# Square sums and factor rows of the norms on TensorE, token halves in the first head, and the last head's output-gate products in its own recursion

## The chip, the cores and the metric

The kernel runs on one core of a Trainium2 chip. The metric is the time of one execution on the device in microseconds (us); the kernel before takes 2332.52 us, the median of three runs (2330.86 to 2333.41). Five engines run side by side, each through its own list of instructions in a fixed order: TensorE (PE: matmuls, PEld: the weight loads beside them), VectorE (DVE), ScalarE (ACT), GpSimd (POOL) and SyncE (SP, which issues most DMAs). An engine that comes to an instruction whose inputs are not there waits, and everything behind it in its list waits too.

## The reference, cut to what matters

```python
def rmsnorm(x, w):
    y = x * lax.rsqrt(jnp.mean(x * x, axis=-1, keepdims=True) + EPS)
    return y * w

def mlstm_mixer(h, ...):                # 4 heads, chunks of 128 tokens, both directions
    proj = h @ w_in                     # q, k, v, output gate, 16 gate columns
    o_gate = sigmoid(proj[..., o3:o4])
    h_fwd, h_bwd = chunkwise recursions over q, k, v and the gates
    hs = h_fwd + h_bwd; hs = hs * lax.rsqrt(mean(hs * hs) + EPS) * norm_w
    return (hs * o_gate) @ w_out

for i in range(2):                      # 1024 tokens, width 1024
    hn = rmsnorm(x, norm_mix_w[i])
    x = x + (mlstm_mixer(hn) if i == 0 else window_attn_mixer(hn))
    x = x + swiglu(rmsnorm(x, norm_ffn_w[i]))      # inner width 2816
return rmsnorm(x, norm_final_w)
```

Everything is in float32. So there are five norms: before the mLSTM (norm 0), before the first feed-forward network (FFN0, norm 1), before the attention (norm 2), before the second (FFN1, norm 3), and at the end.

## The kernel before, in words

**Layout.** `x` lies transposed: eight tiles of 128 features by 1024 tokens. A float32 product is made of three faster ones: both operands are split into a high and a low part (`hnh`/`hnl`, `wh`/`wl`; ACT makes the high part at L187 or L200, DVE or POOL the low part at L201, L205 or L188), and PE runs high-high, low-high and high-low into one PSUM bank.

**A norm.** The factor of a token is a sum over features, that is over partitions. ACT squares the eight `x` tiles; DVE adds the squares into one tile `R` (`norm_square_row`, L285 to L292); PE sums `R` over partitions with one-column matmuls (`norm_sums`, L364); `rsqrt` (L348) makes the factor from the sums by one power on POOL and six small DVE operations, token by token down the partitions (`rcol`); `spread` (L370) turns it into a row over all partitions: DVE multiplies the identity by each column of `rcol`, high and low part (L376, L377), two matmuls with ones follow (L381, L382), ACT copies the result to `R`. The factor is applied to the products, not to their inputs, so matmuls of normed inputs can start before it is known. Norms 1 and 3 are computed while the last output projection before them ends: each finished pair of `x` tiles is made into the FFN's operands (`norm_forms`, L320: `f1`, `f23h`/`f23l`, `f12h`/`f12l`, `f34h`/`f34l`), then squared. The sums and rows are left as two pending steps, which the FFN takes up between its products (`settle`, L441, called at L563 and L574).

**The FFN's start.** `ffn_up` (L536) has seven products of half size per 128 hidden units (`seven`, L525, matmuls at L532). For the first block it runs five products over pairs 0 to 2 first, 45 matmuls, and pair 3 after that.

**The mLSTM.** Each head's inputs come as eight products of 24 matmuls, four for query and key (`qk`: two weights by two token halves) and four for the output gate (`so`), cut into parts of three, and then the values (L476). `m_mix` gives a recursion of steps: `pk` and `pn` matmuls at L212 that wait for DVE and ACT (`cf`, `cp`) and are waited for by them. `weave` (L55) puts the parts of the next head between the steps of the current one. The last head has no next one: its recursion was woven with the output projection of heads 0 and 1 (`out_pair(y01)`, L668), after `take_back` (L708) has fetched and split their kept outputs and `load_x` (L235) has queued the sixteen loads of `x`.

**The order.** The Tile framework's scheduler sets each engine's order from the program's order and a model of its own; buffers come from pools (46 tiles of 128x1032 floats, PSUM banks in phases), so a tile's new use waits for the last reader of the old one.

Of the kernel before, what the change touches and what calls it, by code (L numbers as in the profile page):

```python
# [19 lines left out]
P = 128  # L20
# [61 lines left out]
class Trunk:  # L82
# [58 lines left out]
    def sources(self):  # L141
        h = self.h
        cols = lambda src: [src[:, o:o + D] for o in range(0, src.shape[-1], D)]
        out = [h["m_gate"]]
        for u in range(3 * NH):
# [12 lines left out]
        for u in range(4):  # L158
            att += cols(h["a_out"][u])
        return out + ffn[0] + att + ffn[1]  # L160
# [124 lines left out]
    def norm_square_row(self, d):  # L285
        nc = self.nc
        if not self.seen[0]:
            nc.scalar.activation(self.R, self.x[d], AF.Square)
        else:
            sq = self.unit(name="sq")  # L290
            nc.scalar.activation(sq, self.x[d], AF.Square)
            nc.vector.tensor_tensor(self.R, self.R, sq, op=ALU.add)  # L292
        self.seen = [n + 1 for n in self.seen]

    def norm_direct(self, half):
        nc = self.nc
        V, G = nc.vector, nc.gpsimd
        a, b = (self.slab() for _ in range(2))
        for d in range(KT):
            x = self.xv(d, half)  # L300
            sq = (b if d % 2 else a)[:, d // 2 * HALF:(d // 2 + 1) * HALF]
            if half and d < 6:
                nc.scalar.activation(sq, x, AF.Square)
            else:
                G.tensor_tensor(sq, x, x, op=ALU.mult)
        V.tensor_tensor(a[:, :S], a[:, :S], b[:, :S], op=ALU.add)
        G.tensor_tensor(a[:, S:], a[:, S:], b[:, S:], op=ALU.add)
        yield
        V.tensor_tensor(a[:, :S], a[:, :S], a[:, S:], op=ALU.add)
        V.tensor_tensor(self.Rv(half), a[:, :HALF], a[:, HALF:S], op=ALU.add)  # L310
        yield
# [36 lines left out]
    def rsqrt(self, out, ss, n, tag, w):  # L348
        nc = self.nc
        v = self.t([P, w], F32, tag + "v", 2)  # L350
        g = self.t([P, w], F32, tag + "g", 2)
# [18 lines left out]
    def spread(self, t, n):  # L370
        nc = self.nc
        hi, lo = (self.t2(F32R)[:, :n] for _ in range(2))
        for j in range(n // P):
            o = slice(j * P, (j + 1) * P)
            r = self.rcol[:, t // P + j:t // P + j + 1]
            nc.vector.tensor_scalar(hi[:, o], self.ident, r, None, op0=ALU.mult)  # L376
            nc.vector.scalar_tensor_tensor(  # L377
                lo[:, o], self.ident, r, hi[:, o].bitcast(F32), op0=ALU.mult, op1=ALU.subtract
            )
        rb = self.bank("mx")[:, :n]  # L380
        nc.tensor.matmul(rb, lhsT=self.ones_r, rhs=hi, start=True, stop=False)  # L381
        nc.tensor.matmul(rb, lhsT=self.ones_r, rhs=lo, start=False, stop=True)  # L382
        nc.scalar.activation(self.R[:, t:t + n], rb, AF.Copy)
        return rb
# [51 lines left out]
    def norm_end(self):  # L436
        sums = lambda: [self.norm_sums(half) for half in range(2)]
        rows = lambda: [self.norm_rows(half) for half in range(2)]
        self.pending = [sums, rows]
# [96 lines left out]
    def ffn_up(self, i):  # L536
# [4 lines left out]
        for f in range(NF):  # L541
# [21 lines left out]
            self.settle()  # L563
# [7 lines left out]
            if f:  # L571
                pc = self.bank("mm")
            self.seven(cur, pc, "s1", "t1", **rest)
            self.settle()  # L574
# [93 lines left out]
    def out_pair(self, ys, last=False):  # L668
# [3 lines left out]
        def piece(e, half):  # L672
# [17 lines left out]
            def done(po):  # L690
                x = self.xv(d, half)
                nc.vector.tensor_tensor(x, x, po, op=ALU.add)  # L692
                if last and e % 2 and half:
                    i = e // 2
                    if i == 2:
                        self.first, todo = self.left()
                        for f in todo:
                            f()
                    self.norm_forms(i)
                    for k in (i, i + 4):  # L700
                        self.norm_square_row(k)
                        self.keep_x(k)

# [147 lines left out]
    def m_in(self, hh, t):  # L851
# [4 lines left out]
        def feature(unit, w, half):  # L856
            dst = lambda: t["qk" if unit == 0 else "so"][:, w * S + half * HALF:w * S + (half + 1) * HALF]

            def pairs():
                if w == 0 and half == 0:  # L860
                    t["qk" if unit == 0 else "so"] = self.slab()
                if half == 0:
                    st["w"] = self.w()
                else:
                    self.ahead()
                return self.dense_pairs(st["w"], half)
# [25 lines left out]
        fs = sum((feature(u, w, half) for u in range(2) for w in range(2) for half in range(2)), [])  # L892
        return fs, self.v_parts(value)
# [164 lines left out]
    def mlstm(self):  # L1058
        nc, h = self.nc, self.h
        with ExitStack() as es:  # L1060
# [6 lines left out]
            with self.tc.manual_schedule(engines={mybir.EngineType.Activation}):  # L1067
                sums = [self.norm_direct(half) for half in range(2)]
                for half in range(2):
                    for d in range(KT):  # L1070
                        self.norm_split(d, half)
                        if half and d == 4:
                            next(sums[0])
                    next(gates)
                    next(sums[half])
                next(sums[1])
# [3 lines left out]
            marks = (11, 16, 28, 36, 44)  # L1080
            norms = [lambda: self.norm_sums(0), lambda: self.norm_rows(0), lambda: self.norm_sums(1), lambda: self.norm_rows(1)]
            for i, f in enumerate(ins[0][0]):
                if i in (1, 3, 4, 7):
                    norms.pop(0)()
# [3 lines left out]
            weave(mix[0][0], ins[0][1])  # L1088
            y01, y2 = [[], []], []
            for hh in range(NH):  # L1090
                early, steps, late, y = mix[hh]
                if hh + 1 < NH:
                    weave(steps, ins[hh + 1][0])
                    nxt = mix[hh + 1][0]
                    both = [late[0], nxt[0], late[1], late[2], nxt[1], late[3], late[4], nxt[2], nxt[3]]
                    weave(both, ins[hh + 1][1])
# [10 lines left out]
            self.norm_end()  # L1107
# [247 lines left out]
    def attn(self):  # L1355
# [8 lines left out]
        with self.phase("a", 6, dict(mm=3, sc=2, tp=2, mx=1)):  # L1364
# [45 lines left out]
            self.norm_end()  # L1410
# [98 lines left out]
```

## Time and profile before

| | |
|---|---|
| median of three runs | 2332.52 us |
| the profiled execution | 2334.53 us |
| its span, first to last instruction | 2332.8 us |
| mean granted TensorE clock | 0.982 |
| busy: PE, PEld | 2228.1 us (96%), 1826.9 us (78%) |
| busy: DVE, ACT, POOL | 1421.6 us (61%), 832.8 us (36%), 608.7 us (26%) |

Busy times are shares of the span; the engines overlap. PE has the work that fills the time, so what counts is where PE stands still or runs at its lower clock. The granted clock is given as a share of 2.4 GHz; 0.50 is 1.2 GHz.

### The profile page before, as it was taken

Reading aid. Unit: us, or ns where it says so; the run is one execution under the profiler, and the core shown is the slowest. Engines: PE = TensorE matmul, PEld = TensorE weight load, DVE = VectorE, ACT = ScalarE, POOL = GpSimd, SP = SyncE. Lnnn points to the kernel's source line nnn. Section 1 sums busy time; section 2 is a strip of 40 time slices with the busy share of each in tenths; the row PEclk is TensorE's granted clock in tenths of the full one; section 3 lists DMA queues with packets and bytes.
Section 4 is the critical chain, followed back from the end, with each engine's and each line's share of the span. In section 5 each row is a group of like instructions: output and inputs, shape, how many; then the busy total and the mean of one; then the engine's idle time right before and its main releaser. Section 6 shows DMA issues by size and latency. Waiting matters only on the chain.

```text
span 2332.8 us, 28234 instructions
## 1 busy us (share of the span) xinstructions
PE 2228.1 (96%) x10655; PEld 1826.9 (78%) x10655; DVE 1421.6 (61%) x2603; ACT 832.8 (36%) x1533; POOL 608.7 (26%) x410
## 2 busy tenths in 40 slices
PE   6999998989999999999999998898999999999998
PEld 3889888867888888778878776786788888878887
DVE  5456656678766666592224689878766666653113
ACT  3334445344222222222222577764322222232021
POOL 4312213221111111231343455550111111133043
PEclk9999999998999999999999999999999999999999
DMA  3211114122222222622222444603222222263112
GB/s 114 58 37 46 52 49 145 55 99 82 82 82 82 82 81 77 229 97 86 92 89 85 130 132 135 206 10 116 74 82 81 82 82 82 74 240 119 46 55 73
DMA packets 75961, 216.77 MB, mean 93 GB/s; under 512 B 8320, under 2 KB 14976, under 8 KB 75824
## 3 DMA queue, kind: packets, MB, share of 16 engines
q1 hardware_dynamic: 64216, 177.07, 23.3%
q10 hardware_dynamic: 11608, 37.89, 4.1%
q8 instruction: 84, 1.38, 0.2%
q14 instruction: 53, 0.43, 0.1%
HBM read 159.15 MB, written 55.77 MB: 92 GB/s over the span
## 4 chain that ended last, share of the span: by engine, by line
PE 77%; DVE 8%; issue 5%; DMA 4%; POOL 2%; ACT 2%; SPq 1%; POOLq 0%; ACTq 0%; DVEq 0%
PE mm L532 37%; PE mm L628 18%; PE mm L228 12%; PE mm L476 4%; PE pn L212 2%; DMA raw<-in_a_in_dram 1%; PE sc L1271 1%; POOL wl L188 1%; DVE smd L1286 1%; PE pk L212 1%; DMA slab<-bounce 1%; PE tp L1300 1%; PE mx L1315 1%; ACT e L1280 1%; DVE e L1276 1%
## 5 line engine op out<-in xcount | busy, mean ns | idle before, releaser
L188 POOL TENSOR_TENSOR wl<-raw,wh 128x1024 fp32r<-128x1024 f32 (+2 forms) x96 | 233.7, 2439 | 594.0 <-ACT wh L187 391.2
L628 PE MATMUL mm<-hh,wl 128*128 128x512 f32 (+1 forms) x768 | 289.9, 378 | 4.6 <-POOL wl L188 4.6
L628 PE MATMUL mm<-hh,wh 128*128 128x512 f32 (+1 forms) x768 | 289.0, 379 | 4.3 <-ACT hh L200 3.2
L628 PE MATMUL mm<-hl,wh 128*128 128x512 f32 (+1 forms) x768 | 289.9, 377 | 1.1 <-DVE hl L201 1.1
L579 POOL TENSOR_TENSOR t<-t,R 128x512 f32<-128x512 f32 x44 | 57.4, 1305 | 613.6 <-ACT t L578 613.6
L628 PEld LDWEIGHTS mm<-hh,wh 128*128 128x128 f32 x768 | 145.4, 189 | 34.4 <-ACT hh L200 4.0
L628 PEld LDWEIGHTS mm<-hh,wl 128*128 128x128 f32 x768 | 145.3, 189 | 34.4 <-POOL wl L188 5.9
L628 PEld LDWEIGHTS mm<-hl,wh 128*128 128x128 f32 x768 | 145.5, 189 | 30.3 <-DVE hl L201 1.9
L655 DVE TENSOR_TENSOR x<-x,mm 128x512 f32<-128x512 f32 x80 | 54.6, 685 | 178.2 <-PE mm L628 178.0
L228 PE MATMUL mm<-slab,wh 128*128 128x512 f32 x512 | 152.8, 407 | 6.1 <-ACT wh L187 3.1
L578 ACT ACTIVATE t<-t 128x512 f32<-128x512 f32 x44 | 27.8, 632 | 330.9 <-DVE t L577 330.9
L532 PE MATMUL mm<-f12h,wbh 128*128 128x512 f32 x352 | 138.9, 395 | 0.0
L532 PE MATMUL mm<-f12l,wbh 128*128 128x512 f32 x352 | 138.7, 394 | 0.0
L532 PE MATMUL mm<-f12h,wbl 128*128 128x512 f32 x352 | 138.7, 394 | 0.0
L570 DVE TENSOR_TENSOR t<-mm,t 128x512 f32<-128x512 f32 x44 | 30.4, 691 | 159.9 <-PE mm L532 159.9
L187 ACT ACTIVATE wh<-raw 128x1024 fp32r<-128x1024 f32 (+3 forms) x106 | 102.1, 969 | 71.9 <-DVE hl L201 56.1
L228 PE MATMUL mm<-hnh,wh 128*128 128x512 f32 x416 | 124.6, 399 | 0.9 <-DVE x L655 0.9
L228 PE MATMUL mm<-hnl,wh 128*128 128x512 f32 x416 | 124.5, 401 | 0.0
L228 PE MATMUL mm<-hnh,wl 128*128 128x512 f32 x416 | 124.1, 398 | 0.0
L532 PE MATMUL mm<-f,wah 128*128 128x512 f32 x352 | 113.0, 403 | 10.8 <-DVE x L692 10.8
L532 PE MATMUL mm<-f34h,wd 128*128 128x512 f32 x352 | 117.6, 394 | 0.0
L228 PEld LDWEIGHTS mm<-slab,wh 128*128 128x128 f32 x512 | 95.9, 193 | 26.8 <-ACT wh L187 4.1
(296 smaller groups left out, 5318.7 us busy)
## 6 DMA issues: line engine op xcount, KB each, us to landing
raw<-in_ffn_in_dram SPq DMA_DIRECT2D x88, 512.0 KB
hkeep<-hs ACTq DMA_DIRECT2D x44, 512.0 KB
hraw<-hkeep SPq DMA_DIRECT2D x44, 512.0 KB
raw<-in_ffn_out_dram SPq DMA_DIRECT2D x32, 512.0 KB
raw<-in_m_in_dram SPq DMA_DIRECT2D x24, 512.0 KB
xkeep<-x ACTq DMA_DIRECT2D x24, 512.0 KB
x<-xkeep SPq DMA_DIRECT2D x48, 256.0 KB
bounce<-slab SPq DMA_DIRECT2D x40, 256.0 KB
```

The source lines that it names most:

```text
L187: nc.scalar.activation(hi[:, c], r[:, c], AF.Copy)
L188: (nc.vector if fast else nc.gpsimd).tensor_tensor(lo[:, c], r[:, c], hi[:, c].bitcast(F32), op=ALU.subtract)
L212: self.nc.tensor.matmul(out, lhsT=l, rhs=r, start=start and i == 0, stop=stop and i == len(jobs) - 1,)
L228: self.nc.tensor.matmul(st["ps"], lhsT=l, rhs=r, start=j == 0, stop=j == len(jobs) - 1)
L476: self.nc.tensor.matmul(st[c], lhsT=l, rhs=r, start=j == 0 and a == 0, stop=j == 1 and a == len(jobs) - 1)
L532: self.nc.tensor.matmul(ps, lhsT=l, rhs=r, start=start and j == 0, stop=stop and j == len(jobs) - 1, skip_group_check=True,)
L570: V.tensor_tensor(u2, pb, p1, op=ALU.add)
L578: A.activation(g0, g0, AF.Silu)
L579: G.tensor_tensor(g0, g0, R0, op=ALU.mult)
L628: nc.tensor.matmul(po, lhsT=l, rhs=r, start=j == 0, stop=j == len(jobs) - 1)
L655: V.tensor_tensor(x, x, po, op=ALU.add)
L1271: T.matmul(ps[:, :n], lhsT=lq, rhs=kk[:, j * S + k0 * P:j * S + (k0 + nk) * P], start=j == 0, stop=j == 1,)
```

## The change

1. In norms 1 and 3 the squares of two `x` tiles are added by DVE once per pair and go to PE at once: eight one-column matmuls for each (`norm_columns`), accumulated in one PSUM bank `pss` over five sets (pair 3 gives its two squares unadded). The factors follow in the output projection itself (`norm_factors`, once for all eight columns), and only the rows are left pending. 2. Norm 0 does the same by token halves, all squares on ACT (`norm_half` in place of `norm_direct`). 3. `spread` uses eight float32 matmuls of 128x128 on a broadcast column of `rcol` and the identity, with no DVE work. 4. The first `settle` in `ffn_up` goes; the other moves ahead of its product. 5. The first head's products go by token halves: q and k of half 0, then of half 1; the gates' steps come at other marks. 6. Four of the last head's eight products, those of the output gate, move from head 2's recursion into the first eight steps of head 3's own; `take_back` and `load_x` come after them.

```diff
-    def norm_square_row(self, d):            # and norm_direct: removed
+    def norm_columns(self, sq, t, n, first, last):
+        for j in range(n // P):
+            c = t // P + j
+            self.nc.tensor.matmul(
+                self.pss[:, c:c + 1], lhsT=sq[:, j * P:(j + 1) * P], rhs=self.ones[:, 0:1],
+                start=first and j == 0, stop=last, skip_group_check=True,
+            )
+    def norm_square_pair(self, i):
+        nc = self.nc
+        if i == 0:
+            self.pss = self.bank("mx")
+        sq = [self.unit(name="sq") for _ in range(2)]
+        for q, d in zip(sq, (i, i + 4)):
+            nc.scalar.activation(q, self.x[d], AF.Square)
+        if i < 3:
+            nc.vector.tensor_tensor(sq[0], sq[0], sq[1], op=ALU.add)
+            sq = sq[:1]
+        for q in sq:
+            self.norm_columns(q, 0, S, i == 0, i == 3 and q is sq[-1])
...
+    def norm_factors(self, t, n):
+        a, b = t // P, (t + n) // P
+        self.rsqrt(self.rcol[:, a:b], self.pss[:, a:b], D, "n", b - a)
...
     def spread(self, t, n):
...
+            nc.tensor.matmul(
+                rb[:, j * P:(j + 1) * P], lhsT=self.rcol[:, c:c + 1].broadcast_to([P, P]), rhs=self.ident,
+                start=True, stop=True,
+            )
...
                     self.norm_forms(i)
+                    self.norm_square_pair(i)
                     for k in (i, i + 4):
-                        self.norm_square_row(k)
                         self.keep_x(k)
+                    if i == 3:
+                        self.norm_factors(0, S)
+                        self.pending = [self.norm_all_rows]
...
+        order = [(u, w, half) for u in range(2) for w in range(2) for half in range(2)]
+        if hh == 0:
+            order[1], order[2] = order[2], order[1]
...
-            marks = (11, 16, 28, 36, 44)
+            marks = (16, 20, 30, 38, 46)
...
-                    weave(steps, ins[hh + 1][0])
+                    weave(steps, ins[hh + 1][0] + (ins[hh + 1][1] if hh + 2 < NH else []))
...
-                    backs = [self.take_back(self.ykeep[j], y01[j]) for j in range(2)]
-                    self.load_x(h["x"])
-                    a, b = 4, 6
-                    weave(steps[:a] + backs + steps[a:b])
+                    a, b, o = 4, 8, ins[hh][1]
+                    weave(steps[:a], o[:16])
+                    backs = [self.take_back(self.ykeep[j], y01[j]) for j in range(2)]
+                    weave(steps[a:b], o[16:])
+                    for f in backs:
+                        f()
+                    self.load_x(h["x"])
```

**The order at three places.** On PE, where the mLSTM's last output projection ends and FFN0 begins, before (`mm_5083` is the last projection product, `mm_5156` the first FFN bank; the number at a name's end tells tiles apart):

```order
L228 MATMUL mm_5083<-slab_4674,wh_4953 128x512
L228 MATMUL mm_5083<-slab_4675,wh_4953 128x512
L228 MATMUL mm_5083<-slab_4674,wl_4954 128x512
L532 MATMUL mm_5156<-f_838_4801,wah_4991 128x512 x2
L532 MATMUL mm_5156<-f_838_4801,wal_4992 128x512
L532 MATMUL mm_5156<-f_856_4892,wah_4991 128x512 x2
L532 MATMUL mm_5156<-f_856_4892,wal_4992 128x512
L532 MATMUL mm_5156<-f_886_5010,wah_4991 128x512 x2
```

After, the same place; `mx_4831` is the bank of sums, `sq_5151` and `sq_5152` are the squares of the last pair:

```order
L228 MATMUL mm_5114<-slab_4680,wh_4977 128x512
L228 MATMUL mm_5114<-slab_4679,wl_4978 128x512
L289 MATMUL mx_4831<-ones,sq_5057 128x1 x8
L289 MATMUL mx_4831<-ones,sq_5151 128x1 x8
L289 MATMUL mx_4831<-ones,sq_5152 128x1 x8
L542 MATMUL mm_5211<-f_833_4808,wah_5015 128x512 x2
L542 MATMUL mm_5211<-f_833_4808,wal_5016 128x512
L542 MATMUL mm_5211<-f_853_4909,wah_5015 128x512 x2
```

Three sets of columns now stand between the projection and the FFN's first matmul, which in turn waits for the reader of `mx_4831`; the sums stood 59 rows behind `mm_5156`'s first row before.

On DVE, the last forms of pair 3 and what follows them, before (`R_4737` is the sum of squares, `nv` the first operation of `rsqrt`):

```order
L201 TENSOR_TENSOR f12l_5105<-t_908_5108,f12h_5104 128x1024
L201 TENSOR_TENSOR f34l_5117<-t_909_5109,f34h_5116 128x1024
L292 TENSOR_TENSOR R_4737<-R_4737,sq_5120 128x1024
L292 TENSOR_TENSOR R_4737<-R_4737,sq_5124 128x1024
L570 TENSOR_TENSOR t_933_5265<-mm_5158,t_924_5209 128x512
L352 TENSOR_SCALAR nv_5219<-mx_5214 128x4
L352 TENSOR_SCALAR nv_5234<-mx_5229 128x4
```

After:

```order
L350 SCALAR_TENSOR_TENSOR t_906_5140<-x_4129,nw,t_905_5139 128x512
L201 TENSOR_TENSOR f12l_5136<-t_905_5139,f12h_5135 128x1024
L201 TENSOR_TENSOR f34l_5148<-t_906_5140,f34h_5147 128x1024
L363 TENSOR_SCALAR nv_5173<-mx_4831 128x8
L366 SCALAR_TENSOR_TENSOR ng_5174<-rcol_4745 128x8
L367 TENSOR_TENSOR ng_5174<-ng_5174,nv_5173 128x8
```

The two additions of pair 3 are gone, and `nv` stands right behind the forms.

On PE, the last head's recursion where it meets the output projection of heads 0 and 1, before (`pn` belongs to a step, `mm_4127` is the first product of `out_pair(y01)`):

```order
L212 MATMUL pn_4178<-cp_4096,slab_3906 128x258
L212 MATMUL pn_4194<-vx_3862,slab_3653 128x258
L212 MATMUL pn_4194<-cp_4105,slab_3905 128x258
L212 MATMUL pn_4194<-vx_3865,slab_3653 128x258
L212 MATMUL pn_4194<-cp_4106,slab_3905 128x258
L212 MATMUL pn_4194<-vx_3862,slab_3654 128x258
L228 MATMUL mm_4127<-slab_4067,wh_4123 128x512 x2
L228 MATMUL mm_4127<-slab_4079,wh_4123 128x512
```

After (`mm_4059` is the last output-gate product, `mm_4155` the first of `out_pair(y01)`):

```order
L228 MATMUL mm_4059<-hnh_220,wl_3949 128x512
L228 MATMUL mm_4059<-hnh_224,wh_3948 128x512
L228 MATMUL mm_4059<-hnl_225,wh_3948 128x512
L228 MATMUL mm_4059<-hnh_224,wl_3949 128x512
L212 MATMUL pk_4146<-vx_3587,slab_3792 128x258
L212 MATMUL pk_4146<-vx_3590,slab_3792 128x258
L212 MATMUL pk_4146<-vx_3587,slab_3793 128x258
L228 MATMUL mm_4155<-slab_4098,wh_4055 128x512 x2
L228 MATMUL mm_4155<-slab_4110,wh_4055 128x512
```

Before, the steps follow each other with nothing between; after, each of the first eight steps has twelve output-gate matmuls behind it, and the projection comes behind the last of these.

## Rows read from the trace of the kernel before

**Rows 1.** The page, chain that ended last: its share of the span by engine.
```profile
PE 77%; DVE 8%; issue 5%; DMA 4%; POOL 2%; ACT 2%; SPq 1%; POOLq 0%; ACTq 0%; DVEq 0%
```

**Rows 2.** Windows: length, busy us of PE, PEld, DVE, ACT, POOL; PEclk; DMA.
```profile
50.00:60.00 10.00, 10.00 (x34) 7.86 (x32) 4.45 (x11) 1.78 (x3) 0.00 (x0) 0.72 0.24 67
...
300.00:360.00 60.00, 60.00 (x334) 51.80 (x333) 34.80 (x98) 25.25 (x53) 10.22 (x5) 1.00 0.11 36
...
400.00:415.00 15.00, 10.06 (x36) 7.77 (x35) 8.80 (x19) 6.85 (x14) 9.50 (x6) 0.66 0.42 159
...
425.00:435.00 10.00, 8.14 (x38) 6.79 (x37) 8.42 (x14) 4.43 (x7) 4.75 (x2) 0.83 0.17 66
...
525.00:530.00 5.00, 5.00 (x13) 3.84 (x13) 4.90 (x6) 4.79 (x7) 0.00 (x0) 0.50 0.27 107
...
560.00:565.00 5.00, 5.00 (x15) 3.90 (x14) 3.30 (x4) 2.53 (x3) 0.39 (x1) 0.58 0.27 108
...
600.00:620.00 20.00, 20.00 (x88) 16.22 (x87) 13.74 (x19) 5.23 (x7) 2.60 (x2) 1.00 0.24 79
```

**Rows 3.** Waits of PE: us in total, times, longest one.
```profile
PE mm L532 <- DVE x L692: 10.8, 2, 5.4
...
PE mm L532 <- ACT t L559: 6.8, 2, 3.4
...
PE mx L381 <- DVE t L376: 6.6, 4, 3.1
```

**Rows 4.** Timeline of PE, the two FFN starts: start, us, instruction.
```profile
524.71 1.19 PE L532 MATMUL mm<-f,wah 128*128 128x512 f32 x2 [5.40 <-DVE x L692]
...
541.87 1.84 PE L364 MATMUL mx<-ones,R 128*128 128x1 f32 x16
...
558.85 0.80 PE L532 MATMUL mm<-f23h,wah 128*128 128x512 f32 x1 [3.40 <-ACT t L559]
...
1623.05 1.19 PE L532 MATMUL mm<-f,wah 128*128 128x512 f32 x2 [5.40 <-DVE x L692]
```

**Rows 5.** Windows of line 532 alone: length, PE busy (matmuls), PEld; PEclk; DMA.
```profile
524.00:558.80 34.80, 28.66 (x108) 21.95 (x108) 0.89 0.23 76
```

**Rows 6.** Timeline of DVE, end of the mLSTM out-projection.
```profile
507.05 2.81 DVE L292 TENSOR_TENSOR R<-R,sq 128x1024 f32<-128x1024 f32 x1
...
523.88 0.68 DVE L692 TENSOR_TENSOR x<-x,mm 128x512 f32<-128x512 f32 x1
...
528.02 2.55 DVE L292 TENSOR_TENSOR R<-R,sq 128x1024 f32<-128x1024 f32 x2
...
536.77 1.22 DVE L201 TENSOR_TENSOR f34l<-t,f34h 128x1024 fp32r<-128x1024 f32 x1
```

**Rows 7.** Timeline of ACT, the same stretch.
```profile
536.37 2.00 ACT L291 ACTIVATE sq<-x 128x1024 f32<-128x1024 f32 x2
```

**Rows 8.** Timelines of PE and SP, last head of the mLSTM.
```profile
398.66 0.63 PE L212 MATMUL pk<-vx,slab 128*128 128x258 f32 x3 [0.36 <-DVE cf L987]
...
403.14 0.39 PE L212 MATMUL pn<-vx,slab 128*128 128x258 f32 x1 [2.41 <-ACT slab L1010]
...
408.30 1.22 PE L228 MATMUL mm<-slab,wh 128*128 128x512 f32 x2 [1.18 <-ACT wh L187]
...
380.45 17.76 SPq L240 DMA_DIRECT2D x<-in_x_dram  x16
```

**Rows 9.** Timelines of PE and DVE, first head: factor rows and gate chain.
```profile
49.49 0.76 PE L381 MATMUL mx<-t,ones 128*128 128x512 f32 x1 [3.07 <-DVE t L376]
...
67.76 0.21 PE L796 MATMUL mx<-ident,msmall 64*1 64x64 f32 x1
...
92.97 1.05 PE L907 MATMUL mx<-slab,slab 128*128 128x128 f32 x8
...
58.57 0.21 DVE L763 SCALAR_TENSOR_TENSOR slab<-slab 64x128 f32<-64x128 f32 x1
...
67.10 0.14 DVE L792 COPY msmall<-slab 32x1 f32<-32x1 f32 x1
```

More of the change, by code (lines that the diff above doesn't have):

```diff
@@ L144, in sources @@
         out = [h["m_gate"]]
-        for u in range(3 * NH):
+        for u in list(range(3 * NH - 2)) + [3 * NH - 1, 3 * NH - 2]:
             out += cols(h["m_in"][u])
@@ new lines, in norm_square_pair, with norm_half @@
+    def norm_square_pair(self, i):
+        nc = self.nc
+        if i == 0:
[8 more added lines that the diff above has]
+            self.norm_columns(q, 0, S, i == 0, i == 3 and q is sq[-1])
+    def norm_half(self, half):
@@ L296, in norm_direct @@
         nc = self.nc
-        V, G = nc.vector, nc.gpsimd
-        a, b = (self.slab() for _ in range(2))
+        if half == 0:
+            self.pss = self.bank("mx")
         for d in range(KT):
[L300 to L311, printed above, removed]
+            self.norm_split(d, half)
+        sqs = [self.unit(name="sq") for _ in range(4)]
+        for d in range(KT):
+            o = d % 2 * HALF
+            nc.scalar.activation(sqs[d // 2][:, o:o + HALF], self.xv(d, half), AF.Square)
+        for j, q in enumerate(sqs):
+            nc.vector.tensor_tensor(q[:, :HALF], q[:, :HALF], q[:, HALF:], op=ALU.add)
+            self.norm_columns(q, half * HALF, HALF, half + j == 0, j == 3)
@@ L371, in spread @@
         nc = self.nc
-        hi, lo = (self.t2(F32R)[:, :n] for _ in range(2))
+        rb = self.bank("mx")[:, :n]
         for j in range(n // P):
[L374 to L378, printed above, removed]
-            )
-        rb = self.bank("mx")[:, :n]
-        nc.tensor.matmul(rb, lhsT=self.ones_r, rhs=hi, start=True, stop=False)
-        nc.tensor.matmul(rb, lhsT=self.ones_r, rhs=lo, start=False, stop=True)
+            c = t // P + j
+            nc.tensor.matmul(
+                rb[:, j * P:(j + 1) * P], lhsT=self.rcol[:, c:c + 1].broadcast_to([P, P]), rhs=self.ident,
+                start=True, stop=True,
+            )
         nc.scalar.activation(self.R[:, t:t + n], rb, AF.Copy)
@@ L437, in norm_end, with norm_all_rows @@
         sums = lambda: [self.norm_sums(half) for half in range(2)]
-        rows = lambda: [self.norm_rows(half) for half in range(2)]
-        self.pending = [sums, rows]
+        self.pending = [sums, self.norm_all_rows]
+    def norm_all_rows(self):
+        for half in range(2):
+            self.norm_rows(half)
     def settle(self):
@@ L562, in ffn_up @@
             self.seven(cur, pe, "s4", "b22", **rest)
-            self.settle()
             more()
@@ L572, in ffn_up @@
                 pc = self.bank("mm")
+            self.settle()
             self.seven(cur, pc, "s1", "t1", **rest)
-            self.settle()
             V.tensor_tensor(u2, pc, u2, op=ALU.add)
@@ L862, in pairs @@
                 if half == 0:
-                    st["w"] = self.w()
-                else:
+                    st[w] = self.w()
+                elif hh or unit or w:
                     self.ahead()
-                return self.dense_pairs(st["w"], half)
+                return self.dense_pairs(st[w], half)
             def done(ps):
@@ L890, in value @@
             self.split_scaled(*vx, ps, self.rcol[:, c:c + 1])
-        fs = sum((feature(u, w, half) for u in range(2) for w in range(2) for half in range(2)), [])
-        return fs, self.v_parts(value)
+        order = [(u, w, half) for u in range(2) for w in range(2) for half in range(2)]
+        if hh == 0:
+            order[1], order[2] = order[2], order[1]
+        fs = [feature(*o) for o in order]
+        return sum(fs[:4], []), sum(fs[4:], []), self.v_parts(value)
     def m_mix(self, hh, st, keep):
@@ L1067, in mlstm @@
             with self.tc.manual_schedule(engines={mybir.EngineType.Activation}):
-                sums = [self.norm_direct(half) for half in range(2)]
                 for half in range(2):
[L1070 to L1073, printed above, removed]
+                    self.norm_half(half)
                     next(gates)
-                    next(sums[half])
-                next(sums[1])
             st = [{} for _ in range(NH)]
@@ L1079, in mlstm @@
             mix = [self.m_mix(hh, st[hh], self.ykeep[hh] if hh < NH - 1 else None) for hh in range(NH)]
-            marks = (11, 16, 28, 36, 44)
-            norms = [lambda: self.norm_sums(0), lambda: self.norm_rows(0), lambda: self.norm_sums(1), lambda: self.norm_rows(1)]
-            for i, f in enumerate(ins[0][0]):
-                if i in (1, 3, 4, 7):
+            marks = (16, 20, 30, 38, 46)
+            norms = sum(([lambda h=h: self.norm_factors(h * HALF, HALF), lambda h=h: self.norm_rows(h)] for h in range(2)), [])
+            for i, f in enumerate(ins[0][0] + ins[0][1]):
+                if i in (1, 5, 9, 13):
                     norms.pop(0)()
```

17 lines of the change are left out of this document (3 added, 14 removed).

## The prediction

> **What bounds the kernel now.** I read the page's chain first: three quarters of the chain that ended last is PE's own work, 8% DVE's [rows 1]. So time is lost or won only where PE stands or runs at its lower clock, and the windows show where: from 600 on PE is never idle and passes 88 matmuls in 20 us, 0.23 us each, while in a few stretches it is short of that [rows 2]. The table of PE's waits names the largest in the stretches that the change touches: twice 5.4 us on DVE's additions to `x` and twice 3.4 us on ACT's `t`, at the starts of FFN0 and FFN1 alike [rows 3]. Last I read the timelines around them: the two FFN starts are the same picture 1098 us apart, so that one is worked out and counted twice [rows 4].
>
> After a stop PE pays again: in 525 to 530 the granted clock is 0.50 and 13 matmuls pass instead of 22, and in 560 to 565 it is 0.58 and 15 pass [rows 2].
>
> **The FFN starts (norms 1 and 3).** Before, the first FFN matmul waits only for the last addition to `x` (523.88) and starts at 524.71, though its norm's sums are not made before 541.87; meanwhile DVE and ACT make pair 3's forms [rows 4, 6]. Between there and the end of the second stop at 558.85 PE passes 108 matmuls of L532 [rows 4, 5]. After, by the order, the columns of pair 3's two squares stand ahead of that matmul, and it waits as well for DVE's reading of the sums. The forms of pair 3, which were under its cover, now lie on the path.
>
> How late is that? Before, the last form of pair 3 ends at 536.77 + 1.22 = 537.99, 14.1 us after the last addition began [rows 6]. In between one of two additions of squares goes (2.55/2 = 1.3), so 12.8. ACT squares pair 3 behind those forms: the pair of squares ended at 538.37 [rows 7], 1.3 earlier is 537.1. Eight columns follow: the row of 16 records is both halves, eight columns, 1.84 us [rows 4]; then `nv`. That makes 539.0 if the last addition stays where it is. It moves both ways: DVE's list ahead of it loses an addition (1.3; one took 2.81 [rows 6]) and three sums of weights that come later now (0.6 each by the additions of that size, 0.68 in the row at 523.88), 3.1 at most; PE's list gains two sets of columns inside the projection (3.7), each behind a DVE addition of 1.3 to 2.8. I take half a microsecond earlier, 538.5; the ends are 536 and 545.
>
> From there PE needs 108 x 0.23 = 24.8, some 2.5 for the slow spell after the stop, as at 525 to 530, and 1.8 for `spread` in its new form: no row shows it, but four fp32 matmuls of 128x128 are the eight records of 1.05 us [rows 9], so eight are 1.6 to 2.1. 538.5 + 29.1 = 567.6. Before, the same point is 558.85, and the slow spell behind it (7 matmuls short, 1.6 us) makes it 560.5. A loss of 7.1 at each start, 5 to 13 by the ends, **+14 in all**. The second stop, on `t` of ACT, goes, and is counted: by the order the rows follow 62 matmuls, 14 us, behind the start, and the factors need a few small operations. A gain here needs `nv` by 531, 7 us after the last addition, against forms that alone take longer; I exclude it.
>
> The price of a column rests on that row, 1.84/16 = 0.115 us a record. The Trainium skill, in "TensorE: Matmul & The Clock Gate", section "Back-to-back issue gap", gives matmuls of up to 64 columns a floor of about 25 ns; by it a set would cost 0.4 us, and the start would come some 1.4 us sooner, 11 in all instead of 14. The trace disagrees with that floor and agrees with the page's next section, "LDWEIGHTS (loading the stationary operand)": a load of 128 columns takes 128/1.2 = 107 ns whatever streams behind it.
>
> **The last head.** Before, its recursion runs without other work from 394 on and stops at 403.14 (2.41), 408.30 (1.18) and elsewhere [rows 8]; 400 to 415 has 10.06 busy of 15 at clock 0.66, so 4.9 idle and 10.06 x 0.34 = 3.4 slow [rows 2]. After, 96 output-gate matmuls (22 us) lie between these steps. They are work in any case, so the 8.3 come free. Against it: the sixteen loads of `x` take 17.8 us [rows 8], 1.1 each. Before they went at 380, under cover. After, the tiles they fill are still read by the last output-gate product (the order shows `mm_4059` with `hnh` of the normed input), so they start some 3 us ahead of the projection's first product, and the ninth, wanted by the second product some 9 us later (3, and two products of nine matmuls with the steps between), lands at 11 to 12. SP's list has a later weight of the projection behind them, with 12 products to spare. DVE stands there with the steps' operations behind it: 1.5 back. **-7**, from -11 (the stop of 425 to 435 goes too: 1.9 idle, 1.4 slow [rows 2]) to -1.
>
> **Head 2's recursion** gives those 96 matmuls up. From 300 to 360 PE was busy all 60 us and DVE 34.8 [rows 2]; less 22 PE has 38 left beside DVE's 35 and a few less. The two are near each other, and a step with nothing behind it left gaps of 0.36 [rows 8]: sixteen of them are 5.8, none is 0. I take **+2**.
>
> **The first head.** The new `spread` takes DVE off the rows, and the 3.07 us at 49.49 go [rows 9], with the 2.8 of slow clock in 50 to 60 [rows 2]. But what is late next is the gates: DVE starts their chain at 58.57 and ends it at 67.10, 8.5 us, and PE came to the transposes that read it at 67.76, without a wait [rows 9]. PE now comes there some 7 us sooner, and the chain perhaps 1 (an estimate: its reload from memory follows PE's gate product). So PE waits at that place instead, with a slow spell behind: **0**, from -4 to +3. The columns' extra sets, 1.8 per half, lie in the stretch that PE waits through anyway.
>
> **The other norms.** `spread` in norm 2 and at the end leaves DVE: four waits on it were 6.6 us, 3.07 of them counted [rows 3, 9]; PE pays 1.8 less the two matmuls of 0.23. **-1**, 0 to -3. The moved `settle` and the single factor chain cost nothing: DVE and POOL have idle time in the FFN (13.7 and 2.6 busy of 20 [rows 2]); without that cover it is one chain of six small operations, about a microsecond.
>
> **Sum.** 14 - 7 + 2 + 0 - 1 = +8. The profiled execution was 2334.5 us; its like after is 2342.5. The median of the runs lies 2.0 below the profiled one, so the forecast is 2340.5.
>
> **Rivals.** First, faster: the last head decides. If its second stop goes too (11 in all), `x` comes in time and head 2 keeps pace, the two starts may cost their least, 5 each, and the first head gives 3, the norms 3: 10 - 11 - 3 - 3 = -7, 2325.5. The point from which it decides is where the last head gives more than the two starts cost, with the smaller terms at their best. For it speaks that DVE, 4.90 busy of 5 in 525 to 530 [rows 2], is relieved there; against it, that the forms of pair 3 need their 12.8 us all the same. Second, nothing to see: the starts at 5 to 6 each, the rest as forecast, +1 to +4 on the profile, 2333 to 2337; the DVE additions that PE now waits for speak against it. Third, slower by more: head 2's steps leave their gaps (+6) and the projection's column sets each wait for a DVE addition beside POOL's work, as the one of 2.81 did, 10 per start: 20 - 7 + 6 - 1 = +18, 2350.5. A fourth, that the change doesn't do what it says, has no room: the order shows each move.
>
> **How the numbers follow.** Within 0.2% (4.7 us, about what a measurement of this kernel can tell from no change) means 2327.9 to 2337.2. My forecast (2338 to 2346) has 0.40, the third rival 0.13: slower 0.53. The second has 0.22: same. The first has 0.25: faster. The range that leaves out a tenth on each side goes from 2322, a little under the first rival, to 2354, a little over the third. The forecast's own is 2335 to 2347.
>
> **What would show it.** At FFN0's start PE idles 14 to 17 us, broken only by column sets, up to the `nv` at about 538, and the stop at 555 is gone; the same near 1637. In the last head 400 to 415 is full, with output-gate matmuls between the steps, and the first additions to `x` wait for a load. At 60 PE waits for the gates. It would be wrong if the first FFN matmul came by 531, if the idle time before it stayed at 5 us, or if 300 to 360 showed PE idle by over 6 us.

## The result, and the profile after

The changed kernel takes 2371.06 us, the median of four runs (2368.78 to 2373.49), beside 2331.69 us before (median of four, one run more than above): a ratio of 1.0168 [1.0151, 1.0186], some 39 us slower. The profiled execution took 2371.81 us, its span is 2370.1. The direction was forecast, the size was not: 2340.5 with an upper end of 2354. One execution of experiment 5's kernel ran at a mean granted clock of 0.56 and took 3687 us; its median below leaves that one out.

Where it went is read from when the same work comes, by the first and last start of an instruction's line in both traces:

| start of | before, us | after, us | after minus before |
|---|---|---|---|
| head 0's first scores, q by k (L907, L922 after) | 93.0 | 97.6 | +4.6 |
| the mLSTM's last `pn` matmul (L212) | 453.0 | 449.1 | -3.9 |
| the last addition to `x` of its projection | 523.9 | 527.9 | +4.0 |
| the first matmul of FFN0 | 524.7 | 547.6 | +22.9 |
| the first matmul of its second half (L628, L637) | 965.0 | 980.6 | +15.6 |
| the last attention scores (L1271, L1282) | 1551.4 | 1567.8 | +16.4 |
| the last `f` matmul of FFN1 (L532, L542) | 2046.2 | 2083.9 | +37.7 |
| the last matmul (L628, L637) | 2319.9 | 2357.8 | +37.9 |

The first head loses 5, the recursions win 8.5, and from the last recursion step to FFN0's end 19.5 are lost, to be lost once more, 21.3, at FFN1. The rest is even. PE's waits name it (engine and line, what ended the wait: us in total, times, longest):

```profile
PE mx L289 <- DVE sq L302: 27.0, 6, 9.1
...
PE mx L808 <- DVE msmall L804: 6.5, 1, 6.5
...
PE mx L289 <- ACT sq L300: 6.5, 2, 3.3
...
PE mm L542 <- DVE nv L363: 0.5, 2, 0.3
```

The waits of L532 on `x` and on `t` [rows 3] are gone. In their place the column matmuls (L289) wait 33.5 us, 27.0 of it for DVE's additions of squares and 6.5 for ACT's squares. The FFN's own first matmul waits for `nv` only 0.3: all the time before it is spent at the columns ahead of it. The timeline of PE around FFN0's start (start, us, instruction, idle before it and what ended it), with FFN1's first matmul last:

```profile
493.97 2.01 PE L289 MATMUL mx<-ones,sq 128*128 128x1 f32 x16 [2.81 <-DVE sq L302]
...
510.20 1.95 PE L289 MATMUL mx<-ones,sq 128*128 128x1 f32 x16 [0.39 <-DVE sq L302]
...
533.55 3.58 PE L289 MATMUL mx<-ones,sq 128*128 128x1 f32 x16 [9.09 <-DVE sq L302]
...
540.38 6.99 PE L289 MATMUL mx<-ones,sq 128*128 128x1 f32 x32 [3.25 <-ACT sq L300]
...
547.63 1.22 PE L542 MATMUL mm<-f,wah 128*128 128x512 f32 x2 [0.26 <-DVE nv L363]
...
1668.00 1.22 PE L542 MATMUL mm<-f,wah 128*128 128x512 f32 x2 [0.26 <-DVE nv L363]
```

One set of eight columns is 16 records. The two sets inside the projection take 2.0 us each, near the 1.84 of [rows 4]; the one after the stop of 9.09 takes 3.58, and the last two together 6.99. The windows say why (length, busy us of PE, PEld, DVE, ACT, POOL, the granted clock, DMA):

```profile
300.00:360.00 60.00, 57.66 (x386) 52.34 (x385) 46.53 (x138) 28.34 (x68) 12.80 (x8) 1.00 0.08 26
...
400.00:415.00 15.00, 15.00 (x85) 13.02 (x84) 12.43 (x27) 6.59 (x15) 5.71 (x4) 1.00 0.83 293
...
425.00:435.00 10.00, 7.56 (x42) 6.03 (x41) 9.67 (x19) 4.46 (x11) 5.16 (x3) 1.00 0.00 0
...
480.00:500.00 20.00, 17.19 (x76) 13.62 (x75) 12.24 (x15) 9.96 (x10) 2.39 (x1) 0.91 0.44 157
500.00:520.00 20.00, 18.82 (x82) 14.87 (x81) 16.74 (x20) 7.08 (x7) 3.26 (x1) 0.91 0.13 54
...
525.00:530.00 5.00, 0.00 (x0) 0.00 (x0) 5.00 (x7) 1.77 (x2) 0.00 (x0) 0.64 0.13 51
...
535.00:540.00 5.00, 2.13 (x10) 2.04 (x10) 4.57 (x7) 2.62 (x3) 0.00 (x0) 0.50 0.56 188
...
540.00:545.00 5.00, 4.62 (x22) 4.62 (x22) 0.83 (x1) 2.22 (x3) 0.00 (x0) 0.50 0.03 11
...
560.00:565.00 5.00, 5.00 (x23) 3.93 (x23) 0.00 (x0) 0.60 (x1) 0.00 (x0) 1.00 0.00 0
```

From 525 to 540 PE is busy for 3.6 of 15 us and is granted 0.64, then 0.50, that is 1.2 GHz, and it stays at 0.50 while the columns of pair 3 run (3.5 us a set). At 560 the clock is up and the matmuls pass 23 in 5 us; the slow spell that followed the second stop there [rows 2] is gone with it. DVE over the same stretch:

```profile
491.12 2.79 DVE L302 TENSOR_TENSOR sq<-sq,sq 128x1024 f32<-128x1024 f32 x1
...
527.85 0.68 DVE L701 TENSOR_TENSOR x<-x,mm 128x512 f32<-128x512 f32 x1
...
532.27 1.23 DVE L302 TENSOR_TENSOR sq<-sq,sq 128x1024 f32<-128x1024 f32 x1 [0.67 <-ACT sq L300]
...
539.61 1.22 DVE L201 TENSOR_TENSOR f34l<-t,f34h 128x1024 fp32r<-128x1024 f32 x1
```

The last addition to `x` is at 527.85, where it was at 523.88 [rows 6], though the recursions had ended 3.9 earlier. From it to the last form of pair 3 (539.61 + 1.22) are 13.0 us, the forecast's 12.8. ACT squares pair 3 behind them:

```profile
539.29 1.99 ACT L300 ACTIVATE sq<-x 128x1024 f32<-128x1024 f32 x2
```

Those squares end at 541.28; the columns that read them hold the FFN until 547.63.

In the last head, 400 to 415 is full where it was 10.06 of 15 [rows 2]; 425 to 435 is not (7.56, 8.14 before), but stays at the full clock. Two stops are left; the second stood before too (1.86 us at 429.54), the first did not (PE):

```profile
421.44 0.51 PE L212 MATMUL pk<-vx,slab 128*128 128x258 f32 x2 [1.89 <-ACT slab L200]
...
429.22 0.39 PE L212 MATMUL pk<-vx,slab 128*128 128x258 f32 x1 [2.16 <-DVE slab L201]
```

The loads of `x` start at 401.36, and go out in half the time they took before [rows 8] (SP):

```profile
401.36 9.22 SPq L240 DMA_DIRECT2D x<-in_x_dram  x16
```

No engine's wait in the last head ends with one of them. In the first head the factor rows are made without a wait, and PE stands at the gates, first PE, then DVE:

```profile
70.85 0.26 PE L808 MATMUL mx<-ident,msmall 64*1 64x64 f32 x1 [6.53 <-DVE msmall L804]
```

```profile
61.44 0.28 DVE L775 SCALAR_TENSOR_TENSOR slab<-slab 64x128 f32<-64x128 f32 x1 [1.91 <-DMA slab<-gkeep]
...
70.56 0.14 DVE L804 COPY msmall<-slab 32x1 f32<-32x1 f32 x1
```

### The profile page after: what moved, and what is told of

It reads as the page before. It is cut to its first block, busy times and chain, and to the rows that moved or that the text cites. A ratio compares the mean times of both kernels' runs of the same rounds, so it can differ in the third digit from the quotient of the medians.

```text
span 2370.1 us, 28601 instructions
## 1 busy us (share of the span) xinstructions
PE 2255.2 (95%) x10889; PEld 1859.7 (78%) x10889; DVE 1390.1 (59%) x2503; ACT 839.5 (35%) x1544; POOL 588.1 (25%) x396
## 4 chain that ended last, share of the span: by engine, by line
PE 80%; DVE 9%; DMA 3%; ACT 3%; issue 3%; POOL 2%; SPq 0%; POOLq 0%; ACTq 0%; DVEq 0%
PE mm L542 36%; PE mm L637 17%; PE mm L228 16%; PE mm L486 3%; PE pn L212 2%; PE mx L289 1%; PE sc L1282 1%; PE mx L1326 1%; PE tp L1311 1%; PE pk L212 1%; DVE smd L1297 1%; ACT e L1291 1%; DMA raw<-in_a_in_dram 1%; DVE slab L1152 1%; DVE e L1287 1%
## 5 line engine op out<-in xcount | busy, mean ns | idle before, releaser
L637 PE MATMUL mm<-hh,wh 128*128 128x512 f32 (+1 forms) x768 | 288.3, 377 | 6.6 <-ACT wh L187 3.4
L637 PE MATMUL mm<-hh,wl 128*128 128x512 f32 (+1 forms) x768 | 289.6, 377 | 2.9 <-POOL wl L188 2.9
L637 PE MATMUL mm<-hl,wh 128*128 128x512 f32 (+1 forms) x768 | 289.3, 377 | 1.8 <-DVE hl L201 1.8
L637 PEld LDWEIGHTS mm<-hh,wh 128*128 128x128 f32 x768 | 145.0, 189 | 36.4 <-ACT wh L187 4.3
L637 PEld LDWEIGHTS mm<-hh,wl 128*128 128x128 f32 x768 | 145.1, 189 | 32.5 <-POOL wl L188 4.2
L637 PEld LDWEIGHTS mm<-hl,wh 128*128 128x128 f32 x768 | 144.9, 189 | 31.5 <-DVE hl L201 3.1
L542 PE MATMUL mm<-f12h,wbh 128*128 128x512 f32 x352 | 138.9, 394 | 0.0
L542 PE MATMUL mm<-f12l,wbh 128*128 128x512 f32 x352 | 138.5, 393 | 0.0
L542 PE MATMUL mm<-f12h,wbl 128*128 128x512 f32 x352 | 138.4, 393 | 0.0
L187 ACT ACTIVATE wh<-raw 128x1024 fp32r<-128x1024 f32 (+3 forms) x106 | 102.1, 969 | 71.7 <-DVE hl L201 56.6
L542 PE MATMUL mm<-f34h,wd 128*128 128x512 f32 x352 | 117.5, 394 | 0.0
L542 PE MATMUL mm<-f,wah 128*128 128x512 f32 x352 | 113.1, 403 | 0.5 <-DVE nv L363 0.5
```

The costliest lines, as they stand in the source:

```text
L187: nc.scalar.activation(hi[:, c], r[:, c], AF.Copy)
L542: self.nc.tensor.matmul(ps, lhsT=l, rhs=r, start=start and j == 0, stop=stop and j == len(jobs) - 1, skip_group_check=True,)
L637: nc.tensor.matmul(po, lhsT=l, rhs=r, start=j == 0, stop=j == len(jobs) - 1)
```

## The experiments

Ratios are against the kernel before on the same chip, with their 95% intervals. The experiments ran on three chips; the kernel before took 2331.97 to 2332.89 us on them, so medians of different experiments are compared to about a microsecond.

**1. The changed kernel with the old norms 1 and 3.** Everything else of the change stays.

```diff
                     self.norm_forms(i)
-                    self.norm_square_pair(i)
                     for k in (i, i + 4):
+                        self.norm_square_row(k)
                         self.keep_x(k)
-                    if i == 3:
-                        self.norm_factors(0, S)
-                        self.pending = [self.norm_all_rows]
...
             weave(self.out_pair([y2, y], True))
+            self.norm_end()          # and after attention; both settles as before
```

> The changed kernel with norms 1 and 3 as before (squares added by DVE, sums and rows pending into the FFN, both settles at their old places); the new spread, the first head by halves and the moved output-gate products stay. Theory (the columns that stand ahead of the FFN's first matmul cost some 20 us at each of the two FFN starts): both starts come back, 2371 - 41 = 2330 us, first FFN0 matmul some 4 us before the kernel before has it, about 521. Rival (the loss sits in what else moved, in the first head or in the new spread): 2350 or more, and the first FFN matmul still at 540 or later.

Measured: 2325.21 us, ratio 0.9975 [0.9959, 0.9991]. The loss is gone, and 5 us more than the expectation named. PE at the FFN's start (L385 is the sums, L396 the rows):

```profile
520.32 1.20 PE L552 MATMUL mm<-f,wah 128*128 128x512 f32 x2 [5.40 <-DVE x L712]
...
537.49 1.84 PE L385 MATMUL mx<-ones,R 128*128 128x1 f32 x16
...
545.31 1.05 PE L396 MATMUL mx<-ident,rcol 128*128 128x128 f32 x8
...
550.46 1.13 PE L396 MATMUL mx<-ident,rcol 128*128 128x128 f32 x8 [0.85 <-DVE rcol L378]
```

The first FFN matmul waits 5.40 for `x` again, at 520.32. And the stop of 3.40 behind the rows [rows 4] does not come back: the new `spread` keeps DVE out of them.

**2. The kernel before with the moved output-gate products alone.**

```diff
-        return fs, self.v_parts(value)
+        return fs[:len(fs) // 2], fs[len(fs) // 2:], self.v_parts(value)
...                                   # and weave, backs, load_x as in the change
```

> The kernel before with one part of the change alone: the last head's four output-gate products woven into its own first eight steps, its weights in the new order, x loaded after them. Theory: the last head gives what the milestones of the two traces show, 8 us between the first head's end and the end of the recursions, and nothing later takes it back: 2332 - 8 = 2324 us (2320 to 2328). Rival (what was won there was won by the relief of DVE in the new norms, or is lost again at the FFN start because x comes late): 2330 or more.

Measured: 2325.34 us, ratio 0.9972 [0.9961, 0.9984], a gain of 7.3 where 8 was expected. PE at the FFN's start, with the second stop still there:

```profile
517.62 1.19 PE L532 MATMUL mm<-f,wah 128*128 128x512 f32 x2 [5.43 <-DVE x L692]
...
551.90 0.79 PE L532 MATMUL mm<-f23h,wah 128*128 128x512 f32 x1 [3.40 <-ACT t L559]
```

Before, these stood at 524.71 and 558.85: everything is 7 us earlier and stays so.

**3. The kernel before with the columns alone**, old `spread`, old first head.

```diff
                     self.norm_forms(i)
+                    self.norm_square_pair(i)
                     for k in (i, i + 4):
-                        self.norm_square_row(k)
                         self.keep_x(k)
+                    if i == 3:
+                        self.norm_factors(0, S)
+                        self.pending = [self.norm_all_rows]
```

> The kernel before with the square sums of norms 1 and 3 alone as changed: columns in the output projection, factors from one chain, rows pending, settles at the new places; spread stays with DVE. Theory: 20 us at each FFN start, 2332 + 41 = 2373 us, the first FFN0 matmul at about 551, columns of pair 3 at half clock (about 3.5 us a set of eight). Rival (the loss needs the other parts, for instance the eight fp32 matmuls of the new spread): 2345 or less.

Measured: 2373.92 us, ratio 1.0175 [1.0161, 1.0189]. The whole loss is in this part: the first FFN0 matmul comes at 550.85, and the last sets take 3.57 and, two together, 6.99 us. The second stop is gone here too, with the old `spread`: PE does not idle from 550.85 to 600. PE's waits (L298 is the columns):

```profile
PE mx L298 <- DVE sq L311: 24.7, 6, 9.1
...
PE mx L298 <- ACT sq L309: 6.5, 2, 3.3
```

**4. All columns in the FFN.** The changed kernel; `norm_square_pair` keeps its squares, and the five sets run at the first settle.

```diff
-        for q in sq:
-            self.norm_columns(q, 0, S, i == 0, i == 3 and q is sq[-1])
+        self.late = (self.late if i else []) + sq
...
+    def norm_late(self):
+        self.pss = self.bank("mx")
+        for q in self.late:
+            self.norm_columns(q, 0, S, q is self.late[0], q is self.late[-1])
+        self.norm_factors(0, S)
```

> The changed kernel with all five sets of columns taken out of the output projection and put into the FFN, at the first settle after the 45 matmuls of pairs 0 to 2 and the first matmuls of pair 3; the same number of column matmuls. Theory (it is where the columns stand, not their number): the first FFN0 matmul comes at 519 to 522 again, the columns run at the full clock, five sets of 1.95 us for one of 1.84, so some 8 us more of PE work at each start against before, less what DVE's relief gives at the second stop: 2330 + 2 x (4 to 8) = 2338 to 2346 us. Rival (the column matmuls themselves are the price, wherever they stand): 2358 or more.

Measured: 2349.41 us, ratio 1.0076 [1.0061, 1.0091], between the two. Taking the columns out of the FFN's way gives 22 us back, and 24 against experiment 1 are left. Four more sets at 2.0 are 8 at each start, 16 in all. PE shows where the other 8 are:

```profile
522.44 1.19 PE L545 MATMUL mm<-f,wah 128*128 128x512 f32 x2 [5.42 <-DVE x L705]
...
536.22 10.05 PE L289 MATMUL mx<-ones,sq 128*128 128x1 f32 x64
...
546.13 0.77 PE L545 MATMUL mm<-f12h,wbh 128*128 128x512 f32 x1
...
547.13 3.41 PE L289 MATMUL mx<-ones,sq 128*128 128x1 f32 x16
```

Four sets in a row take 10.05 us and the fifth, behind two matmuls, 3.41. The windows of that stretch:

```profile
535.00:540.00 5.00, 5.00 (x41) 4.73 (x40) 0.00 (x0) 1.70 (x4) 0.00 (x0) 1.00 0.55 199
...
540.00:545.00 5.00, 5.00 (x26) 5.00 (x25) 0.00 (x0) 0.94 (x1) 0.00 (x0) 0.52 0.01 3
...
545.00:550.00 5.00, 5.00 (x23) 4.81 (x23) 0.00 (x0) 0.00 (x0) 0.00 (x0) 0.50 0.00 0
```

PE is busy all the time, and still the granted clock goes from 1.00 to 0.50 while it does nothing but one-column matmuls.

**5. The same columns, spaced.** As experiment 4, but the sets of pairs 0 to 2 go one by one between the FFN's first products of nine matmuls.

```diff
                     self.seven(cur, ps, l, r, stop=False, ks=range(3))
+                    if i_ps in (1, 2, 3) and len(self.late) > 2:
+                        self.norm_late(1)
```

> The kernel with the columns in the FFN, but the sets of pairs 0 to 2 one by one between its first products of nine matmuls, only pair 3's two sets at the settle; the number of matmuls is the same. Theory (five sets in a row made the granted clock fall to 0.50, although PE stood nowhere: 13.5 us for five sets instead of 9.8, and some 3.4 us on the matmuls behind them): with matmuls of 512 columns between them the clock stays up, 7 us less at each start, 2349 - 14 = 2335 us, a set 1.95 us. Rival (one-column matmuls are as dear anywhere, or the clock falls with each set): 2345 or more, sets of 2.5 us and longer.

Measured: 2338.06 us, ratio 1.0027 [1.0016, 1.0038]; 11 us less than in one piece, where 14 was expected. Each set is 1.84 us (PE, then the windows):

```profile
522.73 1.19 PE L549 MATMUL mm<-f,wah 128*128 128x512 f32 x2 [5.42 <-DVE x L712]
...
528.92 1.84 PE L289 MATMUL mx<-ones,sq 128*128 128x1 f32 x16
...
532.79 1.84 PE L289 MATMUL mx<-ones,sq 128*128 128x1 f32 x16
...
544.20 1.84 PE L289 MATMUL mx<-ones,sq 128*128 128x1 f32 x16
```

```profile
535.00:540.00 5.00, 5.00 (x31) 4.38 (x30) 0.00 (x0) 0.33 (x1) 0.00 (x0) 1.00 0.64 213
...
540.00:545.00 5.00, 5.00 (x36) 4.51 (x35) 0.00 (x0) 2.49 (x3) 0.00 (x0) 1.00 0.00 0
```

So the clock's fall in experiment 4 came with the columns in a row. What is left, 13 us above experiment 1 by the medians and 8 between the two profiled executions, is near the price of their number: four more sets of 1.84 at each start are 14.7. That nothing else is in it is not shown.

**6. One set less on the path.** The changed kernel, pair 3's squares added by DVE as well.

```diff
-        if i < 3:
-            nc.vector.tensor_tensor(sq[0], sq[0], sq[1], op=ALU.add)
-            sq = sq[:1]
+        nc.vector.tensor_tensor(sq[0], sq[0], sq[1], op=ALU.add)
+        sq = sq[:1]
```

> The changed kernel with pair 3's two squares added by DVE before their columns, as for the other pairs: one set of eight columns less ahead of the FFN's first matmul, one DVE addition more. Theory (the sets run at half clock there, 3.5 us each, and lie on the path): 3.5 less and 1.2 to 2 more at each start, 2371 - 4 = 2367 us. Rival (only the wait for the squares is on the path, the columns are not): the addition comes on top, 2372 to 2375.

Measured: 2368.83 us, ratio 1.0168 [1.0144, 1.0192]: 2.2 below the changed kernel's median, and not told apart from it by the times (its runs spread over 16 us). PE:

```profile
537.93 3.58 PE L289 MATMUL mx<-ones,sq 128*128 128x1 f32 x16 [9.09 <-DVE sq L301]
...
546.98 3.57 PE L289 MATMUL mx<-ones,sq 128*128 128x1 f32 x16 [5.47 <-DVE sq L301]
...
550.90 1.19 PE L541 MATMUL mm<-f,wah 128*128 128x512 f32 x2 [0.35 <-DVE nv L362]
```

In the trace the end of the way is 537.93 to 550.90, 13.0 us, where it was 14.1 (533.55 to 547.63): the set saves 3.4, the addition takes 2.2 of it back. The theory's direction, half its size; by the times alone this stays open. The start itself, 550.90, is later than the changed kernel's because this execution was 4.5 us later from the first head on, where both have the same code: so much can one trace differ from another.

**7. The two parts that pay.** The kernel before with the moved output-gate products and the new `spread`; first head, square sums and settles as before.

```diff
     def spread(self, t, n):
-        hi, lo = (self.t2(F32R)[:, :n] for _ in range(2))
...
+            nc.tensor.matmul(
+                rb[:, j * P:(j + 1) * P], lhsT=self.rcol[:, c:c + 1].broadcast_to([P, P]), rhs=self.ident,
+                start=True, stop=True,
+            )
```

> The kernel before with two parts of the change: the output-gate products in the last head's own recursion, and spread by eight fp32 matmuls on PE. First head, sums of squares and settles as before. Theory (spread on PE ends the FFN's second stop, which the run with the old norms 1 and 3 no longer shows, and that run gave 4 us back in its first head): 2325 - 4 = 2321 us (2317 to 2323), no wait of 3.4 us behind the factor rows. Rival (the second stop costs nothing in the end, and the first head by halves is free): 2324 to 2327, as with the moved products alone.

Measured: 2319.59 us, ratio 0.9948 [0.9936, 0.9961], the lowest median of all, clear of both kernels though not of experiment 8. PE, with no stop of 3.4 behind the rows (L375), only 0.35 later on:

```profile
516.27 1.19 PE L528 MATMUL mm<-f,wah 128*128 128x512 f32 x2 [5.43 <-DVE x L688]
...
540.92 2.02 PE L375 MATMUL mx<-ident,rcol 128*128 128x128 f32 x16 [0.15 <-DVE rcol L357]
...
550.50 0.50 PE L528 MATMUL mm<-f12h,wbl 128*128 128x512 f32 x1 [0.35 <-DVE wbl L201]
```

It differs from experiment 1 by the first head and norm 0 alone, so these cost 5.6 us there by the medians; the two intervals just touch, and the traces agree: head 0's first scores come at 91.18 here and at 96.45 there.

**8. The gates later**, in experiment 1's kernel.

```diff
-            marks = (16, 20, 30, 38, 46)
+            marks = (16, 28, 38, 46, 54)
```

> The kernel with the old norms 1 and 3 (new spread, first head by halves, moved products), with the gates' steps at parts 28, 38, 46, 54 in place of 20, 30, 38, 46, which puts the transposes 18 matmuls further back on PE. Theory (PE waits 6.2 us for DVE's gate chain only because the transposes stand too early): the wait falls to 2 us, the slow spell behind it with it, 2325 - 5 = 2320 us. Rival (the chain sets when the recursion of head 0 can start, so that PE waits the same time at a later place): 2324 to 2327.

Measured: 2321.54 us, ratio 0.9950 [0.9932, 0.9968], 3.7 below experiment 1 where 5 was expected; the runs spread over 12 us and the two intervals overlap, so the times do not settle it. The transposes (L816) now wait 1.97 and not 6.2:

```profile
75.67 0.21 PE L816 MATMUL mx<-ident,msmall 64*1 64x64 f32 x1 [1.97 <-DVE msmall L812]
```

But in the profiled execution (2324.35 us) nothing of this arrives: head 0's first scores come at 97.72 (96.45 in experiment 1), the mLSTM's last `pn` matmul at 451.6 (448.1) and the first FFN0 matmul at 523.9 (520.3); it gets ahead only behind the attention. So the rival, that PE loses the same time at a later place, stands.

## Why the prediction was wrong

**The mechanism was right and its size was not.** The step that failed is the one on how late FFN0's first matmul comes, "+14 in all" for the two starts: it came to 41 (19.5 and 21.3 by the table, 41 by experiment 3 alone). Two terms of it were mis-sized, and a third was right, all for one start:

- *The last addition to `x`* was put half a microsecond earlier. Counted from the last recursion step it came 7.9 us later. The two sets of columns inside the projection were 4.0 of it, as forecast; the waits for the additions of squares 3.2 (2.81 and 0.39; the first addition took 2.79 us beside POOL's work, as the one of 2.81 in [rows 6]), which only the ends of the range had; and the clock fell behind them, to 0.91 over each of the two stretches of 20 us from 480 to 520 (1.00 before), which was nowhere in the sum. By an estimate from those windows that is 0.09 of 36 busy us, some 3; 2 to 3 us of it all came back elsewhere.
- *The columns behind pair 3's squares* were put at 1.84 us from a row at full clock. After the idle time that the forecast itself described, the clock was 0.50 and a set took 3.5; two sets followed the first square (540.3 + 7.0) where the forecast had one, at full clock, behind the second. From the last addition to the first matmul: 19.8 us measured, 15.1 forecast. The two terms are 8.4 and 4.7 off, 13 at a start and 26 in all, nearly what lies between 14 and 41.
- *What comes after* was right: 2.5 for the slow spell, 1.95 for the rows (1.8 forecast), no second stop.

The upper end of that term, 545, was below what was measured even with the 3.9 us won before (547.6, or 551.5 on the old scale): the bound had been built from the same full-clock row. Experiment 5 bears out that row where the clock is up: 1.84 us for 16 records, 0.115 each. Where the granted clock was 0.50 a record took 0.21 to 0.22 (16 in 3.41 us in experiment 4, in 3.58 in the changed kernel), so the price in the sum was one for the full clock alone. The 25 ns of the Trainium skill ("TensorE: Matmul & The Clock Gate", section "Back-to-back issue gap"), set against it in the prediction, are reached in no run; they are a floor, so the prediction was wrong to read 115 ns as disagreeing with them.

**The last head**: 7 forecast for it and 2 lost in head 2's recursion, 5 net; the table has 8.5, experiment 2 alone 7.3. Head 2's loss was right (57.66 busy of 60 in 300 to 360, where it was 60.00 [rows 2]; 2.3 us). The loads of `x` cost nothing: they took 9.22 us and not 17.8, and the wait counted for them did not come.

**The first head**: 0 forecast, within -4 to +3. It cost 4.6 in the table and 5.6 between experiments 7 and 1. In all six traces with the new first head the scores come at 96.5 to 102.1, in the four with the old one at 91.2 to 93.1. The wait for the gates that was named is there (6.53), but the chain was late as well: its reload landed at 61.44 and it ended at 70.56, where it had been 58.57 and 67.10 [rows 9]. The estimate that the chain would start a microsecond sooner was wrong; the gates' normed rows stand behind a product's eviction now (L886 at 53.20), for which DVE waited 5.71 us. Experiment 8 shows that the length of PE's wait is a matter of where the transposes stand; that a shorter wait there gives time back is not shown.

**The other norms**: -1 forecast. The new `spread` is worth more: about 5.8 us (experiments 2 and 7), in the traces mostly at the FFNs, where the two second stops (6.8) go; the forecast counted these under the columns. Rightly so for the changed kernel: the columns alone remove them (experiment 3), and `spread` cannot do it again. Without it the parts add up, 41.3 - 7.3 + 5.6 = 39.6 beside 39.4 measured.

**The rivals.** The third, slower by more, looked for the loss at the projection's column sets, whose waits were 3.2 us of it, and at gaps in head 2 (6, where 2.3 came); it too left out the clock. The first had the last head decide: that gave 8.5, but the starts cost 41 and not 10, and DVE's relief did not make up for it; with the columns spaced and DVE relieved the kernel is still 13 us behind experiment 1. The sum of the second does not come out as written: two starts at 5 to 6 each with the rest as forecast are +4 to +6, not +1 to +4.

**The signs.** Of those named, the full 400 to 415, the vanished second stop and the wait for the gates came. The idle time at FFN0's start was 12.6 us, a little less than the 14 to 17 named, with 10.6 us of columns in it; no addition to `x` waited for a load.

## What to carry to other kernels

Work that is put ahead of an engine's next independent work in its order takes that work's cover away: before moving a reduction onto the busiest engine, ask what stood behind it that did not need it. Where an idle time is forecast, price what follows it at the lower clock, and let the upper bound contain that. And take a change of several parts apart: here two of its parts were worth 12 us and a third cost 41.

## What the runs showed of the hardware

TensorE's granted clock fell while the engine was busy with one-column float32 matmuls and did not idle. In experiment 4 PE was busy without a gap from 530 to 555, and the granted clock fell from 1.00 to 0.50 while four sets of eight columns ran in a row; in experiment 5 single sets of 1.84 us between products of nine wide matmuls left it at 1.00. Which property of these matmuls it was (the one column, the load before each, the type) no run here tells apart. In the changed kernel a set took 1.95 to 2.0 us at or near the full clock and 3.5 at half. The Trainium skill ("TensorE: Matmul & The Clock Gate", section "Loop structure matters more than you think") calls a loop good whose matmuls stay back-to-back, as dense work, because PE stays warm in it. Experiment 4's columns stood back-to-back, and the granted clock fell to 0.50 all the same; whether the page would call one-column matmuls dense it does not say there.
